# Operands of a matmul stream at two fixed byte offsets, with GpSimd's DMA ring cut to 4 KB

## The chip, the cores and the metric

One core of a Trainium2 chip runs one program. The metric is the device time of one execution in microseconds. Before the change three runs took 1829.79, 1835.62 and 1836.05 us; the median is 1835.62 us.

## The reference, cut to what matters

One step of one decoder layer for 256 prompt tokens and 8 sample tokens together, in float32. The tokens are normed and go through an input projection to 14,368 columns; these feed three groups of heads (windowed attention, a pooling mixer, a gated delta rule with a short convolution); what the heads give, gated, goes through an output projection, and a last norm.

```python
h = rms_norm(x, norm_w)
z = h @ w_in                      # (264, 4096) @ (4096, 14368)
qa, ka, va, ga, ub, gb, qc, kc, vc, gc, ac, bc = split_cols(z)
...
mix = jnp.concatenate([oa * silu(ga), ob * silu(gb), oc * silu(gc)], axis=-1)
y = x + mix @ w_out               # (264, 4096) @ (4096, 4096)
y = rms_norm(y, final_norm_w)
```

The caches (keys and values of the last 2048 positions, 128 MB in all) are outputs too, shifted by one position, and so are the new states of the delta rule.

## The kernel before, in words

All activations lie transposed: a tile has 128 channels on the partitions and the 264 tokens along the row. A projection is made of output tiles of 128 columns, 113 for the input projection (`N_IN`) and 32 for the output projection (`N_OUT`). Each output tile runs over 32 contraction tiles (`NK`), in chunks of 8 (`KC`).

Both operands of a product are split into an upper and a lower part of type float32r. One contraction tile of one output tile is therefore three matmuls, lines 540 to 542: the upper part of the weights by the upper part of x, the upper part of the weights by the lower part of x, the lower part of the weights by the upper part of x. The weights are the operand that is held in TensorE, loaded anew before each matmul (PEld); x, or the mixed heads, is the operand that streams past them, 264 columns of 4 bytes, 1056 bytes of each partition. `rhs` gives the two streamed operands of a contraction tile.

The weights' tiles (`wh0` to `wh3`, `wl0` to `wl3`, 4096 bytes a partition for eight contraction tiles of 512) all begin at 128 modulo 256 bytes. The upper part of x is the tile `xh` and its lower part the tile `xl`, each 32 rows of 1056 bytes; both begin at 128 modulo 256. Since 1056 is 4 x 256 + 32, contraction tile k has its upper and its lower part both at 128 + 32 k modulo 256, a round of eight. The mixed heads lie in rows of 2112 bytes, the upper part in front and the lower part 1056 bytes behind it: tiles `mixc0` to `mixc15`, in the places (called r1 slots) that held x as it came in and then the delta rule's keys (`kt`), and the sixteen rows of `mix`, in the place of `xl`. 2112 is 8 x 256 + 64, so in the output stage contraction tile k has its upper part at 128 + 64 k and its lower part at 160 + 64 k modulo 256, a round of four.

Weights come in by 1 MB loads on SyncE's queue into three buffers (`raw`), ScalarE writes the upper part (cast), VectorE the lower part (subtract); both are issued through line 174. Three chunks are split ahead of the one that TensorE works on. Pieces of the caches' copy, HBM to HBM, are issued behind the loads on the same queue (line 158 for all DMAs).

All the rest (convolution, delta rule, attention, pooling, norms) is done by chains of steps, Python generators, which a planner in `step` advances while the stream's chunks are issued, as far as its estimate of VectorE's and ScalarE's time leaves room. Their matmuls (lines 307 and 311) go into the stream ahead of a chunk's last contraction tile. A chain takes its space from one tile, `arena`, by `get` or `get_all`, and yields until there is enough: how much space there is decides which chains run side by side and in which order their loads stand on SyncE's queue, which works in order. The delta rule for sample tokens (`sample_worker`) is one such pair of chains: loads of the state (`sdT`), of keys (`s_k`), a store and a load of the queries (`s_q`), and a store of the new state (`o_ds`).

GpSimd issues a dozen DMAs itself, for constants; their descriptors are written into a ring in SBUF, whose size is given when the program is made.

Of the kernel before, what the change touches and what calls it, by code (L numbers as in the profile page):

```python
# [12 lines left out]
NP = 256            # prompt tokens  # L13
NB = 8              # sample tokens (one per sequence)
NT = NP + NB
NK = 32             # contraction tiles of the model width
KC = 8              # contraction tiles per chunk
# [10 lines left out]
def tile_plan():  # L28
    """Order of the output tiles of the input projection: (kind, index)."""
    plan = [("ab", 0)] + [("k", h) for h in range(CH)]  # L30
    for h in range(CH):
        plan += [("q", h), ("v", h), ("g", h)]
    for h in range(AH):
        plan += [("qa", h), ("ka", h), ("va", h), ("ga", h)]
    for g in range(4):
        plan += [("u", 2 * g), ("u", 2 * g + 1), ("gb", 2 * g), ("gb", 2 * g + 1)]
    return plan
# [37 lines left out]
class Model:  # L75
    """Estimated times (us) of the engines' queues, and of every column's last write and last use."""
# [7 lines left out]
    def span(self, ap):  # L84
        """The quarters of the partitions and the columns of a tile (the kernel's inputs and outputs are not followed)."""
# [31 lines left out]
    def op(self, eng, dur, outs, ins):  # L117
        t = max(self.t[eng], self.ready(outs, ins))
        # engines take turns at a PSUM bank
# [24 lines left out]
class Meter:  # L144
    """An engine, with an estimate of the time that its instructions take (us)."""
# [33 lines left out]
class Chain:  # L179
    """A generator, the estimated time at which its last step is through, and its products yet to be issued."""  # L180
# [10 lines left out]
class Builder:  # L191
# [17 lines left out]
    def setup_space(self):  # L209
# [4 lines left out]
        self.XH = self.xp.tile([P, NK, NT], F32R, tag="xh", name="xh")  # L214
        self.XL = self.xp.tile([P, NK, NT], F32R, tag="xl", name="xl")
        self.r1 = [self.r1p.tile([P, 2, NT], F32, tag=f"r1_{h}", name=f"xr{h}") for h in range(CH)]
# [29 lines left out]
    def get_all(self, *sizes):  # L246
        """All of them or none, so that no two chains wait for each other's space."""
# [42 lines left out]
    def due(self, loaded):  # L290
        """Until a load can be expected to be there."""
# [7 lines left out]
    def lose(self, t):  # L299
        """Time for ScalarE's tables."""  # L300
# [4 lines left out]
    def mm(self, out, lhsT, rhs, start=True, stop=True):  # L305
        """A side product: it is issued inside a later chunk of the stream."""
# [14 lines left out]
    def flush(self, every=True):  # L321
        """The side products whose operands can be expected to be there."""
# [34 lines left out]
    def setup_const(self):  # L357
        d = self.d
        small = self.pool.tile([P, 1600], F32, name="small")
# [37 lines left out]
    def late_const(self):  # L397
# [4 lines left out]
        # halves: silu(z) = (tanh(z/2) + 1) * z/2  # L402
        self.ts(self.cw, self.cw, 0.5, ALU.mult)
        # buffers of the delta-rule phase
# [12 lines left out]
    def setup_stream(self):  # L417
        self.chunks = []      # (m, first k tile, number of k tiles, load index, offset in the load's tiles)
        self.loads = []       # (m, first k tile, number of k tiles, last chunk served, place, load that frees it)
# [36 lines left out]
    def emit_loads(self, limit=None):  # L456
        """The loads whose place is free."""
# [48 lines left out]
    def rhs(self, m, k):  # L506
        if m < N_IN:
            return self.XH[:, k, :], self.XL[:, k, :]
        t = self.mix[k]
        return t[:, 0:NT], t[:, NT:2 * NT]  # L510

    def main_bank(self, m):
        """The PSUM bank of an output tile, and the tile that had it before."""
# [4 lines left out]
    def emit_main(self, n):  # L518
# [3 lines left out]
        for i in range(nk):  # L522
# [8 lines left out]
            if m == 0:  # L531
                # rows 0 to 63: W's upper part by x; rows 64 to 127: its lower part by x's upper part
# [16 lines left out]
    def split_x(self, k):  # L549
        x = self.r1[k // 2][:, k % 2, :]  # L550
        w = self.nw[:, k:k + 1]
        self.act(self.XH[:, k, :], x, AF.Copy, scale=w)
        self.stt(self.XL[:, k, :], x, w, self.XH[:, k, :].bitcast(F32), ALU.mult, ALU.subtract)

    def square_x(self, q):
        """Squares of four of the k tiles, summed into self.ssum."""
# [51 lines left out]
    def ev_conv(self, kind, h, ps):  # L608
# [31 lines left out]
        if kind == "k":  # L640
            r = self.r1p.tile([P, 2 * NT], F32, tag=f"r1_{h}", name=f"kt{h}")
# [18 lines left out]
    def ev_ab(self, ps):  # L660
# [13 lines left out]
        # a_log -> -exp(a_log)  # L674
# [47 lines left out]
    def decay(self, h, gcb, D):  # L722
        """D[j, t, i] = exp(gc_i - gc_j) for i >= j, else 0."""
# [58 lines left out]
    def invert(self):  # L782
        """T = (I + A)^-1 of the 128 diagonal 32 x 32 blocks, one block per partition."""
# [32 lines left out]
    def assemble(self, hb):  # L816
        """E = T^T of the 128 x 128 tiles, from its 32 x 32 diagonal blocks, in place of U."""
# [90 lines left out]
    def delta(self, h, R, kd, D, o, S, X, sq):  # L908
# [65 lines left out]
        # 128 eps (sum q^2 + eps)  # L974
# [19 lines left out]
        # the last reader of k, U and E has been issued: their place takes the head's output  # L994
        mt = self.r1p.tile([P, 2 * NT], F32R, tag=f"r1_{h}", name=f"mixc{h}")
# [7 lines left out]
    def put_mix(self, mt, base, m, c0, c1):  # L1003
        hi, lo = mt[:, base + c0:base + c1], mt[:, base + NT + c0:base + NT + c1]
# [6 lines left out]
    def sample_tab(self):  # L1011
        """Columns by (head, sequence), then rows on all partitions: e^g, k2 e^g beta, k beta."""
# [737 lines left out]
```

## Time and profile before

| | |
|---|---|
| median of three runs | 1835.62 us (1829.79 to 1836.05) |
| profiled execution, first to last instruction | 1828.2 us |
| fastest run, median, over that span | 1.6 us, 7.4 us |
| TensorE busy | 1801.3 us, 99% |
| VectorE busy | 1298.7 us, 71% |
| ScalarE busy | 850.3 us, 47% |
| mean granted clock of TensorE | 0.995 |
| DMA, mean over the span | 284 GB/s, 519.66 MB |

The profile gives the span of the profiled execution and no other time of it. How to read it: PE are TensorE's matmuls, PEld its weight loads; a matmul's record reaches from its first column to an end that is modelled, and records of matmuls that follow each other overlap. What a matmul costs is therefore the distance from its start to the next one's start, called the interval here. A count in a window takes in every record that touches it, those begun just before it too.

### The profile page before, as it was taken

Reading aid. Unit: us, or ns where it says so; the run is one execution under the profiler, and the core shown is the slowest. Engines: PE = TensorE matmul, PEld = TensorE weight load, DVE = VectorE, ACT = ScalarE, POOL = GpSimd, SP = SyncE. Lnnn points to the kernel's source line nnn. Section 1 sums busy time; section 2 is a strip of 40 time slices with the busy share of each in tenths; the row PEclk is TensorE's granted clock in tenths of the full one; section 3 lists DMA queues with packets and bytes.
Section 4 is the critical chain, followed back from the end, with each engine's and each line's share of the span. In section 5 each row is a group of like instructions: output and inputs, shape, how many; then the busy total and the mean of one; then the engine's idle time right before and its main releaser. Section 6 shows DMA issues by size and latency. Waiting matters only on the chain.

```text
span 1828.2 us, 38217 instructions
## 1 busy us (share of the span) xinstructions
PE 1801.3 (99%) x15120; PEld 1790.3 (98%) x15120; DVE 1298.7 (71%) x3155; ACT 850.3 (47%) x1442; POOL 192.8 (11%) x504
## 2 busy tenths in 40 slices
PE   9999999999999999999999999999999999999996
PEld 9999999999999999999999999999999999999995
DVE  7987879668789788787877778676655654444444
ACT  7644444455455455455544443434333444444442
POOL 1132560421011101111000000000000000000000
PEclk9999999999999999999999999999999999999998
DMA  9788897656787888879888888889888798888873
GB/s 322 263 289 295 272 234 260 237 198 234 262 327 269 286 305 313 304 267 319 323 312 306 313 308 297 284 283 333 306 299 288 274 339 302 295 294 303 297 240 118
DMA packets 109380, 519.66 MB, mean 284 GB/s; under 512 B 25408, under 2 KB 35872, under 8 KB 70272
## 3 DMA queue, kind: packets, MB, share of 16 engines
q1 hardware_dynamic: 108624, 516.71, 80.5%
q8 instruction: 118, 1.93, 0.4%
q0 software_dynamic: 432, 0.50, 0.1%
q14 instruction: 62, 0.51, 0.1%
q10 hardware_dynamic: 144, 0.02, 0.0%
HBM read 499.67 MB, written 152.50 MB: 357 GB/s over the span
## 4 chain that ended last, share of the span: by engine, by line
PE 88%; DVE 5%; DMA 4%; issue 1%; ACT 1%; SPq 1%; DVEq 0%; ACTq 0%
PE mps L540 27%; PE mps L541 27%; PE mps L542 27%; PE sps L307 4%; DVE arena L174 3%; DMA raw<-win 3%; DVE wl L174 2%; PE sps L311 1%; PE sps L541 1%; PE sps L540 1%; PE sps L542 1%; SPq L158 1%; DVE y L174 1%; DMA o_ds<-arena 0%; ACT wh L174 0%
## 5 line engine op out<-in xcount | busy, mean ns | idle before, releaser
L540 PE MATMUL mps<-xh,wh 128*128 128x264 f32 x3456 | 995.3, 288 | 2.0 <-ACT wh L174 2.0
L542 PE MATMUL mps<-xh,wl 128*128 128x264 f32 x3456 | 979.9, 284 | 1.7 <-DVE wl L174 1.6
L174 DVE TENSOR_TENSOR wl<-raw,wh 128x1024 fp32r<-128x1024 f32 (+1 forms) x581 | 704.5, 1214 | 389.7 <-ACT wh L174 382.4
L541 PE MATMUL mps<-xl,wh 128*128 128x264 f32 x3456 | 980.2, 284 | 0.0
L174 ACT CAST wh<-raw 128x1024 fp32r<-128x1024 f32 (+2 forms) x586 | 604.8, 1036 | 611.2 <-PE mps L541 471.7
L540 PEld LDWEIGHTS mps<-xh,wh 128*128 128x128 f32 x3456 | 652.1, 189 | 3.7 <-ACT wh L174 2.5
L541 PEld LDWEIGHTS mps<-xl,wh 128*128 128x128 f32 x3456 | 651.7, 189 | 0.2
L542 PEld LDWEIGHTS mps<-xh,wl 128*128 128x128 f32 x3456 | 648.8, 188 | 2.5 <-DVE wl L174 2.5
L174 DVE SCALAR_TENSOR_TENSOR arena<-arena 128x128 f32<-128x128 f32 (+5 forms) x882 | 264.6, 356 | 10.9 <-DMA arena<-s_k 4.2
L174 ACT ACTIVATE arena<-arena 128x128 f32<-128x128 f32 (+7 forms) x319 | 119.3, 401 | 143.3 <-DVE arena L174 140.8
L542 PE MATMUL mps<-mix,wl 128*128 128x264 f32 x512 | 145.7, 284 | 0.0
L542 PE MATMUL mps<-mixc,wl 128*128 128x264 f32 x512 | 145.7, 284 | 0.0
L540 PE MATMUL mps<-mixc,wh 128*128 128x264 f32 x512 | 145.5, 284 | 0.0
L540 PE MATMUL mps<-mix,wh 128*128 128x264 f32 x512 | 145.5, 284 | 0.0
L541 PE MATMUL mps<-mixc,wh 128*128 128x264 f32 x512 | 144.9, 283 | 0.0
L541 PE MATMUL mps<-mix,wh 128*128 128x264 f32 x512 | 144.8, 283 | 0.0
L174 POOL COPY arena<-arena 128x8 f32<-128x8 f32 (+5 forms) x192 | 67.8, 376 | 450.7 <-DVE arena L174 392.8
L540 PEld LDWEIGHTS mps<-mix,wh 128*128 128x128 f32 x512 | 96.2, 188 | 0.0
L540 PEld LDWEIGHTS mps<-mixc,wh 128*128 128x128 f32 x512 | 96.2, 188 | 0.0
L542 PEld LDWEIGHTS mps<-mixc,wl 128*128 128x128 f32 x512 | 96.1, 188 | 0.0
L542 PEld LDWEIGHTS mps<-mix,wl 128*128 128x128 f32 x512 | 96.1, 188 | 0.0
L541 PEld LDWEIGHTS mps<-mixc,wh 128*128 128x128 f32 x512 | 96.1, 188 | 0.0
(115 smaller groups left out, 1340.9 us busy)
## 6 DMA issues: line engine op xcount, KB each, us to landing
raw<-win SPq DMA_DIRECT2D x214, 1024.0 KB, 7.0
o_wk<-ck SPq DMA_DIRECT2D x128, 511.8 KB, 7.4
o_wv<-cv SPq DMA_DIRECT2D x128, 511.8 KB, 6.8
raw<-wout SPq DMA_DIRECT2D x58, 1024.0 KB, 5.3
arena<-kg SPq DMA_DIRECT2D x32, 320.0 KB, 6.7
arena<-vg SPq DMA_DIRECT2D x32, 320.0 KB, 7.1
arena<-sdT SPq DMA_DIRECT2D x32, 256.0 KB, 4.5
arena<-s_k SPq DMA_DIRECT2D x32, 256.0 KB, 4.5
```

The lines of the kernel that those rows point to most:

```text
L158: return f(*a, **k)
L174: return f(*a, **k)
L307: self.put(lambda: self.t.matmul(out, lhsT=lhsT, rhs=rhs, start=start, stop=stop), out, [lhsT, rhs], 2)
L311: self.put(lambda: self.t.transpose(out, in_, self.ident[:k, :k]), out, [in_], 1)
L540: self.t.matmul(ps, lhsT=h[:, w], rhs=xh, start=(k == 0), stop=False)
L541: self.t.matmul(ps, lhsT=h[:, w], rhs=xl, start=False, stop=False)
L542: self.t.matmul(ps, lhsT=l[:, w], rhs=xh, start=False, stop=(k == NK - 1))
```

## The change: what it does

Rows of the streamed operands become 2304 bytes long (`ROW`, 576 columns, 9 x 256 bytes), with the upper part 8 columns from the row's start (`HI`, 32 bytes) and the lower part 296 columns from it (`LO`, 1184 bytes, 160 modulo 256). x has two tiles of 16 such rows (`x0`, `x1`) instead of `xh` and `xl`, the r1 slots and `mix` have such rows, and all these tiles begin at a multiple of 256 bytes. Every contraction tile thus has its upper part at 32 and its lower part at 160 modulo 256, in both projections. The weights' tiles still begin at 128 modulo 256.

The arena grows from 11,776 to 12,480 columns of 4 bytes, and the tile of constants from 1600 to 1632. The space comes from GpSimd's DMA ring, which shrinks from 16,384 to 4,096 bytes a partition. Comments are taken out, which moves no instruction; lines 540 to 542 become 542 to 544, and line 307 becomes 308.

```diff
-        self.XH = self.xp.tile([P, NK, NT], F32R, tag="xh", name="xh")
-        self.XL = self.xp.tile([P, NK, NT], F32R, tag="xl", name="xl")
-        self.r1 = [self.r1p.tile([P, 2, NT], F32, tag=f"r1_{h}", name=f"xr{h}") for h in range(CH)]
+        self.X = [self.xp.tile([P, NK // 2, ROW], F32R, tag=f"x{i}", name=f"x{i}") for i in range(2)]
+        self.r1 = [self.r1p.tile([P, ROW], F32, tag=f"r1_{h}", name=f"xr{h}")[:, :2 * NT].rearrange("p (a n) -> p a n", a=2)
+                   for h in range(CH)]
...
-            return self.XH[:, k, :], self.XL[:, k, :]
-        t = self.mix[k]
-        return t[:, 0:NT], t[:, NT:2 * NT]
+            t = self.X[k // 16][:, k % 16]
+        else:
+            t = self.mix[k]
+        return t[:, HI:HI + NT], t[:, LO:LO + NT]
...
-        self.act(self.XH[:, k, :], x, AF.Copy, scale=w)
-        self.stt(self.XL[:, k, :], x, w, self.XH[:, k, :].bitcast(F32), ALU.mult, ALU.subtract)
+        hi, lo = self.rhs(0, k)
+        self.act(hi, x, AF.Copy, scale=w)
+        self.stt(lo, x, w, hi.bitcast(F32), ALU.mult, ALU.subtract)
...
-        mt = self.r1p.tile([P, 2 * NT], F32R, tag=f"r1_{h}", name=f"mixc{h}")
+        mt = self.r1p.tile([P, ROW], F32R, tag=f"r1_{h}", name=f"mixc{h}")
...
-                    self.mix2 = self.xp.tile([P, CH, 2 * NT], F32R, tag="xl", name="mix2")
+                    self.mix2 = self.xp.tile([P, CH, ROW], F32R, tag="x1", name="mix2")
...
-ARENA = 11776
+ARENA = 12480
+ROW, HI, LO = 576, 8, 296
+SCRATCH = 4096
...
-    nc = _bacc.Bacc("TRN2", target_bir_lowering=False, num_devices=1)
+    nc = _bacc.Bacc("TRN2", target_bir_lowering=False, num_devices=1,
+                     dynamic_dma_scratch_size=SCRATCH)
```

Apart from the names of x's tiles the order of instructions is the same up to the delta-rule stage. There, on SyncE's queue, where the first two chains of the sample tokens' delta rule begin, stood before (`raw` are the weights' buffers, `arena` the chains' space, `ck` the cache that is copied):

```order
L158 DMA o_wk<-ck 16x8188
L158 DMA raw_81<-win 128x2048
L158 DMA arena<-sdT 128x512
L158 DMA arena<-s_k 128x512
L158 DMA s_q<-small 128x2x4
L158 DMA arena<-s_q 128x512
L158 DMA raw_79<-win 128x2048
L158 DMA o_wk<-ck 16x8188
L158 DMA arena<-s_gc 128x256 x2
L158 DMA arena<-sdT 128x512
L158 DMA arena<-s_k 128x512
```

and stands now:

```order
L158 DMA o_wk<-ck 16x8188
L158 DMA arena<-sdT 128x512
L158 DMA arena<-s_k 128x512
L158 DMA s_q<-small 128x2x4
L158 DMA arena<-s_q 128x512
L158 DMA raw_81<-win 128x2048
L158 DMA arena<-sdT 128x512
L158 DMA arena<-s_k 128x512
L158 DMA arena<-s_q 128x512
L158 DMA arena<-s_gc 128x256 x2
L158 DMA raw_79<-win 128x2048
```

The first chain's four transfers have moved ahead of the load into `raw_81`, and the second chain's ahead of the load into `raw_79` and the cache's copy.

On TensorE, inside a chunk of the same stage, side products of four heads' keys (`kt`) stood between main products before:

```order
L307 MATMUL sps_104<-arena,kt_1553 64x64 x2
L307 MATMUL sps_104<-arena,kt_1709 64x64 x2
L307 MATMUL sps_104<-arena,kt_1879 64x64 x2
L307 MATMUL sps_104<-arena,kt_1985 64x64 x2
L307 MATMUL sps_106<-arena,kt_1055 128x128
```

and now, in the same place, the side products of four other heads, at another step of theirs:

```order
L308 MATMUL sps_104<-arena,kt_2137 32x32 x4
L308 MATMUL sps_104<-arena,kt_2290 32x32 x4
L308 MATMUL sps_104<-arena,kt_2450 32x32 x4
L308 MATMUL sps_104<-arena,kt_2618 32x32 x4
L308 MATMUL sps_106<-arena,kt_1055 128x128
```

The rows of the main products around them are the same in number; what has moved is which side products stand in which chunk.

## Rows read from the trace of the kernel before

**Rows 1.** The page's busy times: us, share of the span, instructions.
```profile
span 1828.2 us, 38217 instructions
...
PE 1801.3 (99%) x15120; PEld 1790.3 (98%) x15120; DVE 1298.7 (71%) x3155; ACT 850.3 (47%) x1442; POOL 192.8 (11%) x504
```

**Rows 2.** The page's chain that ended last, by line.
```profile
PE mps L540 27%; PE mps L541 27%; PE mps L542 27%; PE sps L307 4%; DVE arena L174 3%; DMA raw<-win 3%; DVE wl L174 2%; PE sps L311 1%; PE sps L541 1%; PE sps L540 1%; PE sps L542 1%; SPq L158 1%; DVE y L174 1%; DMA o_ds<-arena 0%; ACT wh L174 0%
```

**Rows 3.** The page's costliest groups, two of the main stream's.
```profile
L540 PE MATMUL mps<-xh,wh 128*128 128x264 f32 x3456 | 995.3, 288 | 2.0 <-ACT wh L174 2.0
...
L542 PE MATMUL mps<-mix,wl 128*128 128x264 f32 x512 | 145.7, 284 | 0.0
```

**Rows 4.** Windows: us, PE busy (records), clock, DMA share, GB/s.
```profile
1387.00:1433.00 46.00, 46.00 (x383) 1.00 0.74 255
1450.00:1800.00 350.00, 350.00 (x2879) 1.00 0.81 285
```

**Rows 5.** Timeline of PE, input projection: start us, us, instruction.
```profile
1400.29 0.28 PE L540 MATMUL mps<-xh,wh 128*128 128x264 f32 x1
...
1400.65 0.28 PE L540 MATMUL mps<-xh,wh 128*128 128x264 f32 x1
...
1401.02 0.28 PE L540 MATMUL mps<-xh,wh 128*128 128x264 f32 x1
...
1402.11 0.28 PE L540 MATMUL mps<-xh,wh 128*128 128x264 f32 x1
...
1402.47 0.29 PE L540 MATMUL mps<-xh,wh 128*128 128x264 f32 x1
...
1403.19 0.28 PE L540 MATMUL mps<-xh,wh 128*128 128x264 f32 x1
```

**Rows 6.** Timeline of PE, output stage, firsts of five tiles.
```profile
1552.23 0.28 PE L540 MATMUL mps<-mixc,wh 128*128 128x264 f32 x1
...
1552.59 0.28 PE L540 MATMUL mps<-mixc,wh 128*128 128x264 f32 x1
...
1552.95 0.29 PE L540 MATMUL mps<-mixc,wh 128*128 128x264 f32 x1
...
1553.33 0.28 PE L540 MATMUL mps<-mixc,wh 128*128 128x264 f32 x1
...
1553.69 0.28 PE L540 MATMUL mps<-mixc,wh 128*128 128x264 f32 x1
```

**Rows 7.** By line, single matmuls: record in ns, and start.
```profile
L541 PE MATMUL mps<-mixc,wh x1: 281/281/281, 1552.4 to 1552.4; 128*128 128x264 f32 x1
...
L541 PE MATMUL mps<-xl,wh x1: 285/285/285, 1402.2 to 1402.2; 128*128 128x264 f32 x1
...
L540 PE MATMUL mps<-xh,wh x1: 285/285/285, 1400.7 to 1400.7; 128*128 128x264 f32 x1
...
L542 PE MATMUL mps<-xh,wl x1: 283/283/283, 1400.9 to 1400.9; 128*128 128x264 f32 x1
...
L541 PE MATMUL mps<-xl,wh x1: 278/278/278, 1401.9 to 1401.9; 128*128 128x264 f32 x1
...
L540 PE MATMUL mps<-xh,wh x1: 290/290/290, 1401.4 to 1401.4; 128*128 128x264 f32 x1
```

**Rows 8.** Windows: PE, PEld, DVE, ACT, POOL busy, clock, DMA share, GB/s.
```profile
357.00:640.00 283.00, 278.21 (x2451) 274.93 (x2450) 221.31 (x624) 146.41 (x343) 43.42 (x134) 0.99 0.74 260
640.00:985.00 345.00, 342.56 (x2838) 341.14 (x2838) 277.69 (x835) 173.04 (x346) 30.18 (x79) 1.00 0.85 305
```

**Rows 9.** The page's count of HBM traffic.
```profile
HBM read 499.67 MB, written 152.50 MB: 357 GB/s over the span
```

**Rows 10.** DMA, 1200 to 1600 us: totals, then one group of issues.
```profile
DMA packets 18864, 122.02 MB, mean 305 GB/s; under 512 B 4113, under 2 KB 5409, under 8 KB 9761
...
o_wv<-cv SPq DMA_DIRECT2D x79, 511.8 KB, 6.7
```

**Rows 11.** Timeline of POOL: GpSimd's first DMA issue.
```profile
1.25 0.75 POOL L158 DMA_DIRECT2D small<-ident  x1 [0.80 <-POOLq L1741]
```

More of the change, by code (lines that the diff above doesn't have):

```diff
@@ L358, in setup_const @@
         d = self.d
-        small = self.pool.tile([P, 1600], F32, name="small")
+        small = self.pool.tile([P, 1632], F32, name="small")
         off = [0]
@@ L640, in ev_conv @@
         if kind == "k":
-            r = self.r1p.tile([P, 2 * NT], F32, tag=f"r1_{h}", name=f"kt{h}")
+            r = self.r1p.tile([P, ROW], F32, tag=f"r1_{h}", name=f"kt{h}")
             self.kt[h] = r
@@ L1003, in put_mix @@
     def put_mix(self, mt, base, m, c0, c1):
-        hi, lo = mt[:, base + c0:base + c1], mt[:, base + NT + c0:base + NT + c1]
+        hi, lo = mt[:, base + HI + c0:base + HI + c1], mt[:, base + LO + c0:base + LO + c1]
         self.s.copy(out=hi, in_=m.ap[:, c0:c1])
@@ L1110, in sample_end @@
             mt = self.mix[h]
-            self.s.copy(out=mt[:, NP:NT], in_=m)
-            self.tt(mt[:, NT + NP:2 * NT], m, mt[:, NP:NT].bitcast(F32), ALU.subtract)
+            hi, lo = mt[:, HI + NP:HI + NT], mt[:, LO + NP:LO + NT]
+            self.s.copy(out=hi, in_=m)
+            self.tt(lo, m, hi.bitcast(F32), ALU.subtract)
             if h % 4 == 3:
@@ L1177, in split_mix @@
         t = self.mix2[:, k - CH]
-        self.s.copy(out=t[:, 0:NT], in_=m.ap)
-        self.tt(t[:, NT:2 * NT], m.ap, t[:, 0:NT].bitcast(F32), ALU.subtract)
+        hi, lo = t[:, HI:HI + NT], t[:, LO:LO + NT]
+        self.s.copy(out=hi, in_=m.ap)
+        self.tt(lo, m.ap, hi.bitcast(F32), ALU.subtract)
         self.rel(m)
@@ L1345, in ev_y @@
         if m == 0:
-            self.y = self.xp.tile([P, NK, NT], F32, tag="xh", name="y")
+            self.y = self.xp.tile([P, NK, NT], F32, tag="x0", name="y")
             self.acc = [self.now(NT), self.now(NT)]
```

## The prediction

> **What bounds the kernel now.** I read the page's busy times first, then its chain, then the stream of matmuls interval by interval, and at last what stands beside it. TensorE has work in flight for 1801.3 of 1828.2 us [rows 1], and the chain that ended last is the three lines of the main stream, about 27% of the span each; what VectorE, DMAs and ScalarE add to it is a few per cent [rows 2]. So the kernel's time is a number of matmuls times an interval. The page's groups give the number: 3456 for each of the three products with x, 512 for each of six groups with the mixed heads [rows 3], together 10,368 and 3,072. The interval is read from windows and starts, not from the length of a record: records overlap, since one lasts about 284 ns and the next begins after 121. In the output stage 350 us hold 2879 records, two of which began before it, so 350 / 2877 = 121.7 ns [rows 4]; in the last part of the input projection 46 us hold 383, three of them begun before, 46 / 380 = 121.1 [rows 4], and one clean round of eight contraction tiles there takes 1403.19 - 1400.29 = 2.90 us for 24 matmuls, 120.8 ns [rows 5]. [...] Nothing is waited for in these rows: the interval is TensorE's own. [...]
>
> **Does the interval follow the byte offset?** In the kernel before, rows of x move by 32 bytes modulo 256 from one contraction tile to the next, and rows of the mixed heads by 64; the section on the kernel gives where they begin. In the output stage one round of four rows takes 1553.69 - 1552.23 = 1.46 us, and the four rows of three matmuls take 0.36, 0.36, 0.38 and 0.36 us, to within the 0.01 us of the view [rows 6]. The first has its upper part at 128 and its lower at 160; the third, the slow one, has them at 0 and 32. Single records say it to the nanosecond. The record of the lower part's product is 281 ns at 160 in the mixed heads and 285 at 160 in x; the upper part's products at 32 in x are 285 and 283; the shortest and longest that I found in a clean round are 278 and 290 [rows 7]. Record and interval move together: a mean record of 284 ns [rows 3] goes with an interval of 121.7, so I take interval = record - 162, an estimate. Then the stream has intervals from 116 to 128 ns, and where in this band one falls goes with the operand's place.
>
> **The change part by part.** *The places.* After it, every upper part is at 32, every lower part at 160, for all contraction tiles. No row of before has this pair, so I bound it. Upper end: today's rows at these residues in x, (285 + 285 + 283) / 3 - 162 = 122.3 ns [rows 7]. Lower end: the shortest record everywhere, 278 - 162 = 116 ns [rows 7]. Between them I take, for the lower part, the middle of 116 and of 119 (281 - 162), because the mixed heads are the rows that are built most like the change, with a lower part at another residue than its upper part. For the two products with the upper part I take the middle of 116 and of 121 (283 - 162), 118.5; I leave aside the 285, and the 290, because each is the first matmul of a row whose residue has just stepped, and after the change no row steps. Together 117.5 + 2 x 118.5 = 354.5 a row, 118.2 ns a matmul. With x that saves 10,368 x (120.8 - 118.2) = 27 us, with the mixed heads 3,072 x (121.7 - 118.2) = 11 us: 38 us. At the lower end it is 10,368 x 4.8 + 3,072 x 5.7 = 67 us, at the upper end a loss of 10,368 x 1.5 + 3,072 x 0.6 = 17 us.
>
> *What then comes late.* With 118.2 for 121, a chunk of 24 matmuls passes in 2.84 us instead of 2.90. VectorE was busy for 277.69 of 345 us in the heaviest long stretch, 80%, and would be at 82%; DMA engines were at 0.85 there and would be at 0.87 [rows 8]. Both hide it. If VectorE's cover were gone, a chunk would wait for its split, and TensorE behind it; I let the idle time below stand for that.
>
> *The arena.* 704 columns more (11,776 to 12,480) let two sample chains hold their state at once. On SyncE's queue the second chain's loads now stand one load of weights behind the first's, where before the loads of weights and cache copies stood between, and one load of weights has moved behind the first chain's four transfers, one of which stores a row of queries and the next of which reads it back; on TensorE the side products of two sets of heads swap places, between the same main rows. SyncE waits in order, so a load of weights behind them comes later, and the split, and then TensorE. What is at stake is TensorE's idle time in the delta-rule stage: 283.00 - 278.21 = 4.8 us and 345.00 - 342.56 = 2.4 us [rows 8]. I take no change, with 7 us either way.
>
> *The ring.* GpSimd issues a dozen DMAs, the first at 1.25 us in 0.75 us [rows 11], nine of them at the start. They bring constants that are first used when the first six output tiles are through, after some 540 matmuls, 65 us. With a ring a quarter as long an issue may have to wait until one before it has landed; even if each of nine waited 5 us, all would be there at about 50 us. Nothing. The split of x over two tiles, the wider rows of the r1 slots and 32 columns more of constants add no instruction and no wait to the stream.
>
> *Sum.* 1828.2 - 38 = 1790 us of span. The median of the three runs is 7.4 us over that span and the fastest 1.6 us; the change is the same for both, so I forecast 1835.6 - 38 = **1798 us**.
>
> [...] The rows show intervals that differ by residue. [...] Second, HBM: the page of the profile counts 652 MB read and written, 357 GB/s over the span [rows 9]. [...]
>
> **The rivals.** *Unchanged.* The pattern by contraction tile could belong to the weights, not to x: their rows step by 512 bytes and repeat after eight tiles as x's do, and after four the mixed heads' pattern repeats as well. Then the new places do nothing, 1835.6 us, 1829 to 1843 with the arena. For it: the periods agree. Against it: the lower part's record at the same tile (the first of a chunk) is 278 in x and 281 in the mixed heads [rows 7], and other intervals stand at equal tiles. The HBM ceiling would end here too (1822 + 7); I give both 18%.
>
> *Slower.* The interval belongs to the residue alone, and 32 is a bad one: 285, 283 at 32 in x, 285 at 160 in x [rows 7]. Every row then takes 3 x 122.3 = 367 ns, where the mean today is 362 to 365, because good residues no longer make up for bad ones. +17 us, 1853 us; it decides as soon as the mean of the three is over 121.0. For it: the row at 32 in x, 1400.65 to 1401.02, is 0.37 us, longer than that at 160, 1402.11 to 1402.47, 0.36 [rows 5]. Against it: the same residue has 281 and 285 at 160, so the residue alone does not set it. 18%.
>
> [...] 22%.
>
> **How the numbers follow.** Forecast (117 to 119.5 ns) 42%, much faster 22%, unchanged 18%, slower 18%. Less than 0.5%, 9 us, can't be told from no change here. Faster by more: 42 + 22 + 2 of the unchanged = 66%; same 17%; slower 17%. The range reaches from 1750, some 40% of the way from 1769 to 1721, to 1848, most of the way to the slower rival; about 2 in 10 stay out. The forecast's own range is 1780 to 1817.
>
> **What will show it.** Right: in the output stage 350 us hold some 2960 main matmuls instead of 2877, and all rows of three take the same time, with one record length for each of the three products and no round of four or eight. The count of main matmuls is the same. Wrong in its cause: rows that still differ by tile with the residues fixed. Wrong in its size: one length for each product, but not 279 to 281. Wrong beside it: idle time of TensorE in the delta-rule stage over 14 us, or a split that is waited for in the output stage.

## The result and the profile after

The changed kernel takes 1860.3 us, median of 4 runs (1858.72 to 1862.66), where the kernel before took 1835.84 beside it (4 runs, 1829.79 to 1836.9): a ratio of 1.0141 with a 95% interval of 1.0125 to 1.0158. It is slower. A second measurement, with 18 runs of before, gave 1.0105 (1.0087 to 1.0124), so the change costs 1.0 to 1.4%, some 19 to 25 us. The forecast was 1798 us.

The page of the changed kernel answers to [rows 1 to 3]: TensorE still has work in flight for 98% of the span, the same 15,120 matmuls are on it, and the records of the main stream are one to two ns longer. The three lines of the stream are now L542, L543 and L544.

```profile
span 1858.5 us, 38231 instructions
...
PE 1826.0 (98%) x15120; PEld 1815.1 (98%) x15120; DVE 1300.1 (70%) x3155; ACT 849.0 (46%) x1442; POOL 197.9 (11%) x504
...
PE mps L543 26%; PE mps L542 26%; PE mps L544 25%; DVE arena L174 4%; DMA raw<-win 4%; PE sps L308 4%; DVE wl L174 2%; ACT wh L174 1%; PE sps L312 1%; PE sps L543 1%; PE sps L544 1%; PE sps L542 1%; DVE y L174 1%; ACT arena L174 0%; POOL arena L174 0%
...
L542 PE MATMUL mps<-x,wh 128*128 128x264 f32 x3456 | 1002.2, 290 | 0.0
...
L544 PE MATMUL mps<-mix,wl 128*128 128x264 f32 x512 | 145.9, 285 | 0.0
```

The windows answer to [rows 4, 8]. In the output stage 350 us hold 2848 records, two of them begun before: 350 / 2846 = 123.0 ns, where it was 121.7. In the two stretches of the middle (where the delta rule and the other chains run) TensorE is idle for 278.00 - 275.13 = 2.9 us and 422.00 - 413.23 = 8.8 us.

```profile
362.00:640.00 278.00, 275.13 (x2414) 272.74 (x2413) 219.30 (x626) 145.92 (x352) 39.28 (x129) 0.99 0.75 261
640.00:1062.00 422.00, 413.23 (x3351) 409.64 (x3350) 332.11 (x1037) 199.67 (x397) 39.37 (x88) 1.00 0.83 297
...
1482.00:1832.00 350.00, 350.00 (x2848) 350.00 (x2848) 168.23 (x179) 151.44 (x182) 0.00 (x0) 1.00 0.79 282
```

By line, from 1500 to 1790 us, durations stand as shortest, median and longest. With every residue fixed, records of one product still run from 282 to 288, or 283 to 291 ns; only the round of four contraction tiles of [rows 6] is gone.

```profile
L542 PE MATMUL mps<-mix,wh x395: 282/284/288, 1503.0 to 1790.0; 128*128 128x264 f32 x198
```
```profile
L543 PE MATMUL mps<-mix,wh x394: 283/285/291, 1503.1 to 1789.7; 128*128 128x264 f32 x197
```

I also cut each trace at the same main matmuls (by their starts) and split each part into matmuls that the next one follows within 135 ns, longer ones, and side products. For the whole stream: 1648.1 us in 13,614 intervals of 121.06 ns before, 1666.5 in 13,584 of 122.68 after (+18.4 us); longer ones 53.4 and 62.0 (+8.6); side products 108.6 and 111.7 (+3.1). The first cause is thus the interval itself, and something smaller stands beside it, less than these sums say, since the trace before is of the shortest execution (experiment 9).

### The profile page after: what moved, and what is told of

The parts are those of the page before. It is cut to its first block, busy times and chain, and to the rows that moved or that the text cites. A ratio compares the mean times of both kernels' runs of the same rounds, so it can differ in the third digit from the quotient of the medians.

```text
span 1858.5 us, 38231 instructions
## 1 busy us (share of the span) xinstructions
PE 1826.0 (98%) x15120; PEld 1815.1 (98%) x15120; DVE 1300.1 (70%) x3155; ACT 849.0 (46%) x1442; POOL 197.9 (11%) x504
## 4 chain that ended last, share of the span: by engine, by line
PE 84%; DVE 7%; DMA 4%; ACT 2%; issue 2%; POOL 0%; SPq 0%; DVEq 0%; ACTq 0%; POOLq 0%
PE mps L543 26%; PE mps L542 26%; PE mps L544 25%; DVE arena L174 4%; DMA raw<-win 4%; PE sps L308 4%; DVE wl L174 2%; ACT wh L174 1%; PE sps L312 1%; PE sps L543 1%; PE sps L544 1%; PE sps L542 1%; DVE y L174 1%; ACT arena L174 0%; POOL arena L174 0%
## 5 line engine op out<-in xcount | busy, mean ns | idle before, releaser
L542 PE MATMUL mps<-x,wh 128*128 128x264 f32 x3456 | 1002.2, 290 | 0.0
L543 PE MATMUL mps<-x,wh 128*128 128x264 f32 x3456 | 991.0, 287 | 0.0
L544 PE MATMUL mps<-x,wl 128*128 128x264 f32 x3456 | 985.2, 285 | 0.0
L543 PEld LDWEIGHTS mps<-x,wh 128*128 128x128 f32 x3456 | 657.2, 190 | 0.2
L542 PEld LDWEIGHTS mps<-x,wh 128*128 128x128 f32 x3456 | 653.0, 189 | 1.1
L544 PEld LDWEIGHTS mps<-x,wl 128*128 128x128 f32 x3456 | 650.7, 188 | 0.1
L174 DVE SCALAR_TENSOR_TENSOR arena<-arena 128x128 f32<-128x128 f32 (+4 forms) x882 | 264.2, 355 | 10.3 <-DMA arena<-s_k 3.8
L543 PE MATMUL mps<-mix,wh 128*128 128x264 f32 x512 | 146.8, 287 | 0.0
L543 PE MATMUL mps<-mixc,wh 128*128 128x264 f32 x512 | 146.7, 287 | 0.0
L542 PE MATMUL mps<-mixc,wh 128*128 128x264 f32 x512 | 146.0, 285 | 0.0
L542 PE MATMUL mps<-mix,wh 128*128 128x264 f32 x512 | 146.0, 285 | 0.0
L544 PE MATMUL mps<-mixc,wl 128*128 128x264 f32 x512 | 145.9, 285 | 0.0
L544 PE MATMUL mps<-mix,wl 128*128 128x264 f32 x512 | 145.9, 285 | 0.0
L174 POOL COPY arena<-arena 128x8 f32<-128x8 f32 (+5 forms) x192 | 75.0, 413 | 461.3 <-DVE arena L174 401.8
L542 PEld LDWEIGHTS mps<-mix,wh 128*128 128x128 f32 x512 | 96.4, 188 | 0.0
L542 PEld LDWEIGHTS mps<-mixc,wh 128*128 128x128 f32 x512 | 96.4, 188 | 0.0
L543 PEld LDWEIGHTS mps<-mixc,wh 128*128 128x128 f32 x512 | 96.3, 188 | 0.0
L543 PEld LDWEIGHTS mps<-mix,wh 128*128 128x128 f32 x512 | 96.3, 188 | 0.0
L544 PEld LDWEIGHTS mps<-mixc,wl 128*128 128x128 f32 x512 | 96.1, 188 | 0.0
```

Source lines behind the costliest of these rows:

```text
L174: return f(*a, **k)
L542: self.t.matmul(ps, lhsT=h[:, w], rhs=xh, start=(k == 0), stop=False)
L543: self.t.matmul(ps, lhsT=h[:, w], rhs=xl, start=False, stop=False)
L544: self.t.matmul(ps, lhsT=l[:, w], rhs=xh, start=False, stop=(k == NK - 1))
```

## The experiments

**1. The change with the old arena.** The arena sets the order of the work; with 11,776 columns every engine has before's order, in the trace too, and only the places and the ring are new.

```
-ARENA = 12480
+ARENA = 11776
```

> The change with the arena at 11,776 columns as before: new byte offsets, old order of all instructions (ring still 4 KB). Theory A (byte offsets make the intervals longer): interval of the main matmuls 122.7 ns as in the changed kernel, time 1835.8 + 13,500 x 1.6 ns = 1858 us less what the new order cost, 1852 to 1858. Rival B (the new order in the delta-rule stage and the ring cost the time): 1834 to 1840 with the interval near 121.

Measured: 1851.43 us (1849.38 to 1853.81), ratio 1.0062 (1.004 to 1.0084). Mean interval 122.68 ns, the same as with the whole change. The places cost about 11 us by themselves.

**2. The kernel before with the new arena and ring.** Old places, new order.

```
-ARENA = 11776
+ARENA = 12480
...
-    nc = _bacc.Bacc("TRN2", target_bir_lowering=False, num_devices=1)
+    nc = _bacc.Bacc("TRN2", target_bir_lowering=False, num_devices=1, dynamic_dma_scratch_size=4096)
```

> The kernel before with the arena at 12,480 columns and the 4 KB ring: old byte offsets, new order of all instructions. Theory A: interval 121.1 ns, time 1836 plus the new order's own price, 1836 to 1844. Rival B: 1855 to 1862 with the interval at 121.

Measured: 1844.32 us (1841.02 to 1848.75), ratio 1.0029 (1.0016 to 1.0043). Mean interval 121.06 ns, as before. So the order (or the ring) costs some 5 us with no help from the places. What waits is seen in the middle, from 362 to 1065 us, by engine, line, what was waited for, us in all, times, longest. With the new order side products wait for operands from ScalarE and GpSimd, here and in the changed kernel:

```profile
PE sps L311 <- ACT arena L174: 2.6, 1, 2.6
...
PE sps L311 <- POOL arena L174: 1.3, 1, 1.3
```
```profile
PE sps L312 <- POOL arena L174: 2.0, 1, 2.0
...
PE sps L312 <- ACT arena L174: 1.9, 1, 1.9
PE sps L308 <- ACT arena L174: 0.8, 1, 0.8
```

Such waits take 5.6 us here, 4.7 in the changed kernel and 3.5 in its second trace (experiment 4), against 0.5 at most in the eight traces with the old order. Those wait longer for the split of the weights instead, 2.5 to 7.5 us against 1.3 at most with the new order; in experiment 1:

```profile
PE mps L544 <- DVE wl L174: 3.2, 5, 0.8
PE mps L542 <- ACT wh L174: 2.4, 1, 2.4
```

The sum of all waits does not tell the orders apart: 10.2 to 17.6 us with the new one, 6.9 to 16.1 with the old. The 16.1 are experiment 7's, where side products waited longest for VectorE:

```profile
PE sps L311 <- DVE arena L174: 9.4, 6, 4.3
```

So the waits show that the order changed what TensorE waits for, and not where the 5 us are lost.

**3. The stream by itself, 64 fixed pairs.** Nothing runs beside TensorE. Groups of 96 matmuls go round eight rows of x, the weights at 128 modulo 256 bytes as in both kernels; h is the upper part's residue, l the lower part's; px and pm have the moving residues that x and the mixed heads have in the kernel before.

```
for which, off in PATS[pat](k):
    at = w0 // 4 + which * 1088 + (k % 8) * 128
    nc.tensor.matmul(ps[:, :NT], lhsT=W[:, at:at + 128],
                     rhs=X[:, off // 4:off // 4 + NT], ...)
```

> The stream alone: groups of 96 matmuls of 264 columns, weights loaded before each as in the kernel, weights at 128 modulo 256, no split, no loads beside it; it leaves out all the rest of the computation. 64 groups hold the upper operand at h and the lower at l for all rows (h, l in steps of 32 bytes), and two groups have the rounds of the kernel before (32 k, and 64 k with the lower part 32 further). Theory A1 (the residue of each operand to the weights sets the interval, traffic of other engines does not matter): rounds of before 120.8 and 121.7 ns, pair (32,160) 122.7, other pairs spread over some 116 to 126, and at least one pair under 119. Rival A2 (a fixed pair is no better than a round, whatever the pair): all 64 within 121 to 124. [...]

Measured, settled part of each group: px 120.84 and pm 121.7 ns, what the whole kernel before has in the input projection and in the output stage (120.8 and 121.7). So the other engines' traffic did not lengthen the interval here. The 64 fixed pairs go from 120.0 to 126.7 ns; ten of them stand at 120.0, and all but the longest are at 123.2 or less. None is under 120.0: the expectation of one under 119 missed. The pair of the change went at 122.2. (The 126.7, of both parts at 224, did not come again in experiment 8.) The groups' busy time (96 intervals and one overhang of about 0.16 us) shows it roughly:

```profile
L1659 PE MATMUL h224l224w<-x,w 128*128 128x264 f32 x96 | 12.3, 288 | 0.0
...
L1659 PE MATMUL h032l160w<-x,w 128*128 128x264 f32 x96 | 11.9, 286 | 0.0
...
L1659 PE MATMUL pm<-x,w 128*128 128x264 f32 x96 | 11.8, 284 | 0.0
...
L1659 PE MATMUL px<-x,w 128*128 128x264 f32 x96 | 11.8, 284 | 0.0
L1659 PE MATMUL h032l192w<-x,w 128*128 128x264 f32 x96 | 11.7, 284 | 0.0
```

**4. The changed kernel again**, measured beside experiments 5 to 7; no edit.

> The changed kernel itself, beside the next three, so that old and new offsets with old and new order of the work stand in one comparison. Theory O (offsets and order add up): the earlier runs gave the offsets with the old order 1.0062 and the new order with the old offsets 1.0029, so about 1.009 to 1.010 is left to be added here, against the 1.0141 first measured. Rival I (the two act on each other, or the first figure is the true one): 1.013 to 1.016. Mean interval of the main matmuls 122.7 ns either way.

Measured: 1857.19 us, ratio 1.0105 (1.0087 to 1.0124). The parts, 1.0062 and 1.0029, give 1.0091, so they add up within the interval. That the first comparison gave 1.0141 is not explained; it had four runs of before, whose times go from 1829.8 to 1844.5 in the measurements up to here.

**5. The lower part at 192 modulo 256.** With the old arena.

```
-ROW, HI, LO = 576, 8, 296
+ROW, HI, LO = 576, 8, 304
-ARENA = 12480
+ARENA = 11776
```

> The changed kernel with the lower part at column 304 (192 modulo 256 bytes) instead of 296 and with the old arena of 11,776 columns, which gives the old order of the work. In the stream by itself the pair of 32 and 192 went at 120.0 ns a matmul, the pair of 32 and 160 at 122.3. Theory P (the pair of residues alone sets the interval, and what the other engines do adds nothing): 120.0 to 120.4 ns a main matmul in the whole kernel, 13,600 x (120.2 - 121.06) = -12 us against the kernel before, so about 0.992 to 0.996. Rival W (the interval hangs on the residues of the weights' tiles too, which the stream by itself had at one place only): 121.5 to 123 ns, 1.003 to 1.008, like the run with the new offsets and the old order.

Measured: 1829.19 us (1828.6 to 1833.56), ratio 0.995 (0.9934 to 0.9966): faster than both kernels. The mean interval is 120.21 ns. Eight columns, 32 bytes, are worth 1.1% to the same kernel with the same order (1.0062 in experiment 1), 21 us. In the output stage every record of a product now has one length:

```profile
L542 PE MATMUL mps<-mix,wh x400: 284/284/284, 1503.2 to 1785.0; 128*128 128x264 f32 x134
```
```profile
L543 PE MATMUL mps<-mix,wh x400: 284/284/284, 1503.3 to 1785.2; 128*128 128x264 f32 x134
```
```profile
L544 PE MATMUL mps<-mix,wl x400: 281/281/281, 1503.4 to 1785.3; 128*128 128x264 f32 x134
```

**6. The upper part at 128 modulo 256**, the lower part left at 160, old arena.

```
-ROW, HI, LO = 576, 8, 296
+ROW, HI, LO = 576, 32, 296
-ARENA = 12480
+ARENA = 11776
```

> The changed kernel with the upper part at column 32 instead of 8, so that the parts stand at 128 and 160 modulo 256 bytes, and with the old arena (the old order). Only the upper part is moved; the lower part stays where the change put it. Theory P (the pair alone): 120.0 to 120.4 ns as in the stream by itself, 0.992 to 0.996. Rival L (the lower part at 160, which had the longest interval of the three products in the changed kernel, 123.6 ns, is what is bad): 121.5 to 123 ns, 1.003 to 1.008.

Measured: 1831.21 us (1826.12 to 1835.19), ratio 0.9955 (0.9937 to 0.9973); 120.22 ns. So 160 is no bad place for the lower part; with the upper part at 128 it has the shortest interval that is left, 116.4 ns, and the product behind it 123.6, 360.0 for the three. Its records in the output stage are shorter than those of experiment 5, at the same interval (281 for L542 too):

```profile
L543 PE MATMUL mps<-mix,wh x407: 281/281/281, 1499.8 to 1790.0; 128*128 128x264 f32 x136
```
```profile
L544 PE MATMUL mps<-mix,wl x406: 284/284/284, 1499.9 to 1789.7; 128*128 128x264 f32 x136
```

**7. The ring alone.** The kernel before, with a ring of 4 KB.

```
-    nc = _bacc.Bacc("TRN2", target_bir_lowering=False, num_devices=1)
+    nc = _bacc.Bacc("TRN2", target_bir_lowering=False, num_devices=1,
+                     dynamic_dma_scratch_size=4096)
```

> The kernel before with one edit, the DMA ring of 4 KB; arena, offsets and order as before. Theory S (the schedule's new order carries the 0.3% that the old offsets with the new order showed): 1.000, within 0.0015. Rival R (the smaller ring makes GpSimd wait when it issues its DMAs, and that carries it): 1.002 to 1.004, with longer stretches in which POOL waits before its DMA issues.

Measured: 1837.9 us, ratio 0.9996 (0.9984 to 1.0009). The ring costs nothing in time, and experiment 2's 0.29% is the order's. That it is shorter can be seen: GpSimd's ninth issue waits 0.70 us until the first has landed.

```profile
6.42 0.52 POOL L158 DMA_DIRECT2D small<-al  x1 [0.70 <-DMA small<-ident]
```

**8. The stream by itself: weights moved, other widths.** As in experiment 3, with groups of 480 matmuls (or 192).

```
nc.tensor.matmul(ps[0:M, :N], lhsT=W[:, at:at + M],
                 rhs=X[:, off // 4:off // 4 + N], ...)
```

> Only the stream of main matmuls by itself, nothing else runs; the output is not computed. Groups of 480 matmuls (192 where another width or fewer weights' columns are tried), each with its own name. Theory P (only the streamed operand's residues): 122.3 for the pair of 32 and 160, 120.0 for 32 and 192 and for 128 and 160, 126.7 for 224 and 224, the same for weights at 0, 32, 64, 128 and 192 modulo 256 bytes. Rival W (residues of weights count as well): another interval where the weights are moved, by 1 ns or more. [...]

Measured, with the same streamed operand at 32 and 192: 120.06 ns with weights at 128, 121.12 at 0, 122.23 at 64. At 32 and 160: 122.2 at 128, 121.1 at 0, 121.8 at 32, 122.2 at 64 and at 192. The weights' place counts as much as the operand's, and each of the moved groups has the interval of that pair of experiment 3 that stands as far from the weights modulo 256 (121.1 for 160 and 32, 121.8 for 128 and 0, 122.2 for 96 and 0). Busy time of the groups, the first four with 480 matmuls:

```profile
L1658 PE MATMUL w064f_192t<-x,w 128*128 128x264 f32 x480 | 58.8, 285 | 0.0
...
L1658 PE MATMUL f_224t<-x,w 128*128 128x264 f32 x480 | 58.6, 284 | 0.0
...
L1658 PE MATMUL w000f_192t<-x,w 128*128 128x264 f32 x480 | 58.3, 284 | 0.0
...
L1658 PE MATMUL f_192t<-x,w 128*128 128x264 f32 x480 | 57.8, 283 | 0.0
...
L1658 PE MATMUL n512t<-x,w 128*128 128x512 f32 x192 | 44.8, 395 | 0.0
...
L1658 PE MATMUL n384t<-x,w 128*128 128x384 f32 x192 | 34.0, 338 | 0.0
...
L1658 PE MATMUL m032t<-x,w 128*32 128x264 f32 x192 | 23.2, 282 | 0.0
L1658 PE MATMUL n256t<-x,w 128*128 128x256 f32 x192 | 23.0, 282 | 0.0
...
L1658 PE MATMUL m064n128t<-x,w 128*64 128x128 f32 x192 | 11.7, 223 | 0.0
```

One expectation on the pairs missed: both parts at 224 (`f_224t`), named with 126.7, went at 121.7 through all 480 matmuls, where the group of experiment 3 had 126.7 through its 96 (12.3 us of busy time there), with the same operands' addresses and the clock at 1.00 in both. So one set of addresses can settle at two intervals. The program has other groups ahead of it and another output tile; which of these decides was not tried. The other pairs and rounds that stand in both streams (32 and 160, 32 and 192, 128 and 160, 0 and 0, px and pm) came again to 0.1 ns.

The interval grows with the columns streamed: 118.7 ns for 256 columns, 120.0 for 264, 126.7 for 272, 146.7 for 320, 176.0 for 384, 232.4 for 512. That is 0.454 to 0.466 ns a column. Twice the 118.7 of 256 columns is 237.4, 5.0 more than the 232.4 of 512, so a fixed part would be some 5 ns by these two (an estimate). With 32 columns of weights for 128 the interval of 264 columns is 120.02 still: fewer columns of weights did not shorten it.

**9. The kernel before again**, for a second trace.

> The kernel before once more, for a second trace: how far its stalls and side products differ from one execution to the next. Theory: main matmuls under 136 ns at 121.06 ns again, 1648 us in sum, and the rest (53.4 us of longer intervals, 108.6 us of side products) some 5 to 10 us more than in the trace before, whose execution was the shortest of the four. Rival: the rest is the same within 2 us.

Measured: 1838.47 us. The short intervals are 121.06 ns and 1647.1 us in sum again; the longer ones take 61.8 us for 53.4. The trace ahead of the prediction was of the shortest execution. TensorE's idle time in the middle was 3.4 and 10.0 us here:

```profile
362.00:592.00 230.00, 226.64 (x2034) 223.52 (x2033) 177.63 (x497) 119.17 (x287) 36.34 (x111) 1.00 0.74 259
592.00:1065.00 473.00, 462.96 (x3809) 458.42 (x3808) 376.35 (x1167) 230.22 (x466) 36.89 (x102) 1.00 0.84 299
```

With a second trace, the parts of the span can be compared (us between the starts of main matmuls; the fifth part ends with the last matmul of all):

```
main matmuls             1-2700  to 4300  to 7700  to 10900  to the last
before                    349.9    231.8    452.9     410.3       357.7
before again              350.5    233.4    459.2     410.3       357.7
ring alone (7)            351.3    233.8    464.4     410.3       357.7
old places, new order (2) 350.9    235.1    462.3     409.5       357.7
changed                   355.3    236.6    463.5     415.5       361.5
changed again (4)         354.9    236.3    461.7     415.5       361.5
old arena (1)             354.6    232.9    461.8     415.9       361.4
lower part at 192 (5)     349.4    233.7    457.8     408.1       352.8
upper part at 128 (6)     350.7    231.3    463.8     408.3       352.8
```

The first, fourth and fifth part hardly move from one execution to the next, and there the places show: 1118.5 us before, 1131.9 with the change's places, 1110.3 and 1111.8 with the two better pairs. The middle (the second and third) goes from 684.7 to 698.2 us with the old order whatever the interval, and has 697.4 to 700.1 with the new one. The second part alone keeps the orders apart: 231.3 to 234.4 us in the eight traces with the old order (233.3 and 234.4 in experiments 10 and 11), 235.1 to 236.6 in the three with the new one.

The clock is part of the middle's spread, but not of the order's cost. Behind a stretch with TensorE idle for 2.4 of 7.5 us the granted clock fell from 1.00 to 0.50, and the 3.4 us of the second row hold 15 matmuls, where 28 would pass at 121 ns, some 1.6 us lost (an estimate). In the middle that came once in the trace before, twice in the changed kernel's and in experiment 7's, and not in experiments 2's and 9's:

```profile
600.00:607.50 7.50, 5.08 (x40) 4.65 (x38) 1.75 (x3) 2.63 (x4) 0.00 (x0) 1.00 0.91 297
607.50:610.90 3.40, 3.25 (x15) 3.25 (x16) 2.89 (x10) 0.86 (x4) 0.30 (x1) 0.50 1.06 440
```

**10. The weights moved in the whole kernel.** Experiment 1 with a tile of 128 bytes ahead of the weights' tiles, taken off behind them.

```
+        self.pool.tile([P, 32], F32, name="pad")
         self.H = [self.pool.tile([P, KC * 128], F32R, ...
...
-        small = self.pool.tile([P, 1632], F32, name="small")
+        small = self.pool.tile([P, 1600], F32, name="small")
```

> The changed kernel with the old arena (old order), x and mixed heads at 32 and 160 modulo 256 bytes as in the change, and all tiles of the weights moved by 128 bytes, from 128 to 0 modulo 256. Theory D (what counts is the distance modulo 256 bytes between the weights that are loaded and the operand that is streamed): 32 and 160 against weights at 0 is the same as 160 and 32 against weights at 128, which went at 121.1 ns in the stream by itself, as did this pair against weights at 0: 121.1 to 121.6 ns in the kernel, 0.998 to 1.002. Rival S (the place of the streamed operand alone counts): 122.7 ns and 1.005 to 1.008, as with weights at 128.

Measured: 1842.41 us, ratio 1.0029 (1.0013 to 1.0044); 121.51 ns over the whole stream, 121.1 in the output stage. The streamed operand is where the change puts it, and the interval is 1.2 ns shorter. That its place alone counts is refuted. The time is a little above the 0.998 to 1.002 that theory D gave.

**11. Experiment 5 with the weights moved by 64 bytes.**

```
+        self.pool.tile([P, 16], F32, name="pad")
         self.H = [self.pool.tile([P, KC * 128], F32R, ...
...
-        small = self.pool.tile([P, 1632], F32, name="small")
+        small = self.pool.tile([P, 1616], F32, name="small")
```

> The faster kernel with the lower part at 192 modulo 256 bytes (upper part at 32), with the weights' tiles moved by 64 bytes, from 128 to 192 modulo 256. Theory D (the distance to the weights): this is the pair of 224 and 128 against weights at 128, which went at 122.2 ns in the stream by itself: 122.2 to 122.7 ns in the kernel, all that the place had gained is lost, 1.004 to 1.008. Rival S (the streamed operand alone): 120.2 ns and 0.993 to 0.997 as with weights at 128.

Measured: 1839.58 us, ratio 1.0003 (0.9992 to 1.0014): the gain of experiment 5 is gone. But the interval is neither theory's: 121.6 ns with x, and 120.0 in the output stage. Theory D failed for the mixed heads. One window of 310 us in the output stage tells the kernels apart; intervals are 310 / (records - 2). Before, changed, experiment 5, experiment 10 and this one, 121.7, 122.9, 120.0, 121.1 and 120.0 ns:

```profile
1480.00:1790.00 310.00, 310.00 (x2550) 310.00 (x2550) 150.60 (x160) 134.43 (x161) 0.00 (x0) 1.00 0.83 287
```
```profile
1480.00:1790.00 310.00, 310.00 (x2524) 310.00 (x2523) 149.19 (x158) 133.09 (x160) 0.00 (x0) 1.00 0.85 304
```
```profile
1480.00:1790.00 310.00, 310.00 (x2586) 310.00 (x2585) 152.93 (x163) 136.25 (x162) 0.00 (x0) 1.00 0.83 293
```
```profile
1480.00:1790.00 310.00, 310.00 (x2562) 310.00 (x2562) 151.43 (x162) 135.08 (x161) 0.00 (x0) 1.00 0.84 297
```
```profile
1480.00:1790.00 310.00, 310.00 (x2585) 310.00 (x2585) 155.11 (x167) 138.25 (x167) 0.00 (x0) 1.00 0.85 302
```

**12. The stream by itself, with the kernel's layout.**

```
-    for which, off in PATS[pat](k):
-        at = w0 // 4 + which * 1088 + (k % 8) * 128
+    for which, off in ((0, pat[0]), (0, dl + pat[1]), (1, pat[0])):
+        at = w0 // 4 + which * dw // 4 + (k % 8) * 128
+        off += stride * (k % 8)
```

> Only the stream of main matmuls by itself; the output is not computed. Groups of 480 matmuls, each with its own name. Asked is why the pair of 32 and 192 against weights at 192 went at 120.0 ns with the mixed heads and at 121.6 ns with x in the whole kernel, where the distance modulo 256 bytes to the weights gave 122.2. Names beginning with k have the kernel's layout (rows of 2304 bytes, the lower part 1024 bytes after the upper one's cell, the weights' lower parts 16384 bytes behind the upper ones); with p that of the first stream (2560, 1280, 4352); with q a mixture. Theory H (address bits above 256 count as well, so the equivalence holds only within one layout): ke (192; 32, 192) 120.0 to 120.3, pe 122.0 to 122.4, and one of q tells which of the three distances does it. Rival T (the layout is the same and it is the other traffic in the kernel that moved it): ke and pe alike, 122.0 to 122.4, and kb and pb 120.0 both.

Measured: with the kernel's layout 122.96 ns for the change's places (ka), 120.0 for experiment 5's (kb), 120.0 for 6's (kc), 121.11 for 10's (kd), 120.0 for 11's (ke). All five are what the output stage of the whole kernel has (122.95, 120.0, 120.0, 121.1, 120.0). The addresses of x were laid out in no stream: with the places of 11 the input projection takes 121.6 ns where ke has 120.0, which stays open. The places of 11 in the layout of the first stream (pe) take 122.2, and each single step from the kernel's layout takes it there: the lower part 256 bytes further (qa), rows of 2560 for 2304 (qb), the weights' lower parts 12,032 bytes nearer (qc), or all weights 256 bytes further (qe). The pair of 224 and 128 with the weights at 128 (kf), as far from them modulo 256 as ke's and in the same layout, takes 122.2 too. So address bits above 256 count as well.

```profile
L1653 PE MATMUL kat<-x,w 128*128 128x264 f32 x480 | 59.2, 285 | 0.0
...
L1653 PE MATMUL pet<-x,w 128*128 128x264 f32 x480 | 58.8, 285 | 0.0
...
L1653 PE MATMUL qet<-x,w 128*128 128x264 f32 x480 | 58.8, 285 | 0.0
L1653 PE MATMUL kdt<-x,w 128*128 128x264 f32 x480 | 58.3, 284 | 0.0
...
L1653 PE MATMUL kbt<-x,w 128*128 128x264 f32 x480 | 57.8, 283 | 0.0
...
L1653 PE MATMUL ket<-x,w 128*128 128x264 f32 x480 | 57.8, 283 | 0.0
L1653 PE MATMUL kct<-x,w 128*128 128x264 f32 x480 | 57.8, 282 | 0.0
```

## Why the prediction was wrong

**The bound and the lever** were right. The kernel is a number of matmuls times an interval, the interval follows addresses (if not always one value for one set, experiment 8), and the places alone move the time both ways: 1.0062 with the change's pair, 0.995 with another.

**The step that failed is "the places".** The prediction took 118.2 ns from a band of 116 to 122.3; it is 122.7, just beyond the upper end. Three things in that step were wrong. First, the lower end: it priced each matmul by the shortest record that some matmul has. Intervals in a round are give and take. Experiment 6 has a 116.4 in every round and a 123.6 behind it, 360.0 for the three; no fixed pair of 64 has a mean under 120.0. The sum of a round is what can be had, and 120.0 was its floor in every layout tried: at most 10,368 x 0.84 + 3,072 x 1.7 = 14 us were there to be won, not 38 or 67. Second, "interval = record - 162": experiments 5 and 6 have the same interval of 120.0 with records of 284, 284, 281 and 281, 281, 284. Third, the 285s and the 290 were put aside as effects of a step in residue. With nothing stepping, records of up to 288 and 291 ns remained, with medians of 284 and 285.

**The rival that came true is "slower", by its number (122.3 ns, 1853 us), not by its mechanism.** Places of 32 and 160 are not bad: the lower part at 160 goes with 120.0 when the upper part is at 128, and the upper part at 32 when the lower is at 192, or when weights and layout stand otherwise (experiments 5, 6, 11). It is the arrangement of three addresses, those of the weights, the upper and the lower part, that moves the round (120.0 to 122.96 ns in experiment 12). That is also what the rival "unchanged" was near: the weights' place does count (experiments 8 and 10), though they were not the pattern's owner by themselves. What in the chip makes the weights' address and the streamed operand's act together was not measured.

**The weights' place.** The rows of experiments 8 and 10 have the same streamed bytes at two intervals, by the weights' place alone: 120.06 and 122.23 ns in the stream by itself, 122.68 and 121.51 in the kernel. The prediction asked of the weights only the step, not where they begin.

**The arena** was costed at nothing, 7 us either way. It costs 5.3 us by experiment 2 (0.29% of 1839.4), 5.8 between the medians of experiments 1 and 4, which is within the bounds. The sign named for it, idle time over 14 us, was too coarse: it is 2.9 + 8.8 us after and 4.8 + 2.4 in the trace before [rows 8], while the second trace of before (experiment 9) has 13.4 and that of the ring alone, with before's order, 16.3. Which of the moved loads or side products does it was not tried: what TensorE waits for changed, the sum of its waits did not (experiment 2), and the cause of the 5 us stays open.

**The ring** was right: a wait of 0.70 us appears on GpSimd, and hides (0.9996, experiment 7).

**The sum and the range.** The interval's rise is 13,600 x 1.62 = 22 us, but the places cost 11 to 12. The parts of the span say where the rest is: 13.4 us are lost in the three even parts, and nothing that can be told from the spread in the middle. That waits there, for side chains and splits, take the longer interval in would fit, but was not tried. The prediction let each nanosecond count in full over the whole stream. (Its 10,368 and 3,072 matmuls, together 13,440, leave out 384 that the page lists with another output, 13,824 in all, 1 us of the 38.) The range's lower end was taken part of the way to 1721 us, a time that no run shows: no mean interval in any of the streams by themselves is under 120.0 ns at 264 columns, and the fastest execution took 1826.12 us (experiment 6). The range ended at 1848, short of its own rival at 1853, and the rival was priced without the arena's 7 us: 1853 + 7 = 1860 was in the text in two pieces that were never added. That this meets the 1860.3 measured is luck: by the experiments the pieces are 11 to 12 us and 5, not 17 and 7.

**The signs.** The output stage holds 2848 matmuls in 350 us where 2960 were named; records differ within each product, which was named as wrong in cause if by tile, and is here a round that does not fit the tiles (in experiment 1's trace the records repeat after nine matmuls, in a chunk of 24).

**The ceiling by HBM** of 1822 us, to which the rival "unchanged" adds 7, is a term that no run shows. The page counts 357 GB/s over the span [rows 9], and from 1200 to 1600 us the trace has more: (122.0 + 41.4) / 400 = 408 GB/s, with the copies from HBM to HBM counted twice, an estimate from [rows 10]. The shortest span of a run is 1824.4 us (experiment 6).

## What to carry to other kernels

Where a stream of matmuls is the bound, measure it by itself with the addresses that the kernel will have (weights, operands and row length alike), before a layout is chosen: here it gave the output stage's interval to 0.1 ns for five layouts, and 32 bytes decided between +0.6% and -0.5%. Measure it in more than one order, too, since one pair had two intervals (126.7 and 121.7 ns). Take the price of such a stream from the mean of a whole round, never from its shortest member (116.4 ns in a round whose mean is 120.0, experiment 6). Where two costs of one change can go wrong the same way, add their bad ends before the range is closed.

## What was not expected of the hardware

- The interval of a matmul of 264 columns with a load of 128 columns of weights went from 120.0 to 123.2 ns by where its operands begin (experiment 3, 63 of 64 pairs). The 64th, both parts at 224 with the weights at 128, stood at 126.7 ns there and at 121.7 in experiment 8.
- From 256 columns on, to 512, a streamed column takes 0.454 to 0.466 ns (118.7 ns for 256, 232.4 for 512, experiment 8), and at 264 columns 32 columns of weights for 128 change nothing (120.0; 64 of them gave 121.0).
- With 64 columns streamed and 128 of weights the spacing was 111.7 ns at a granted clock of 1.00, with 192 streamed it was 111.7 as well, and with 128 streamed and 64 of weights 60.0 (experiment 8): in these three it went with the columns of weights, not with those streamed.
- In the group of 64 columns streamed and 128 of weights, with TensorE busy throughout, the granted clock fell from 1.00 to 0.50; it stayed there through the group of 128 columns and was back at 1.00 once the one of 192 was under way (us, PE and PEld busy, DVE, ACT, POOL, clock):

```profile
780.00:790.00 10.00, 10.00 (x88) 10.00 (x87) 0.00 (x0) 0.00 (x0) 0.00 (x0) 1.00 0.01 2
790.00:810.00 20.00, 20.00 (x98) 20.00 (x97) 0.00 (x0) 0.00 (x0) 0.00 (x0) 0.51 0.00 1
...
870.00:880.00 10.00, 10.00 (x92) 10.00 (x91) 0.00 (x0) 0.00 (x0) 0.00 (x0) 1.00 0.01 2
```
